# Moving GpSimd's second exit drain ahead of the take of the barrier's arrivals

## The chip, the cores and the metric

One core of a Trainium2 chip. The time is device microseconds (us) of one execution. The "span" is the time from the first to the last recorded instruction of the one execution that was profiled; the measured time of that same execution is 1.78 us longer (82.27 and 80.488 us for the kernel before).

## The reference

A row-wise L2 normalisation of a 1024 x 4096 f32 matrix:

```python
def reference(x, axis, eps):          # x: 1024 x 4096 f32, axis -1, eps 1e-12
    norm = np.sqrt(np.sum(x ** 2, axis=axis, keepdims=True) + eps)
    return (x / norm).astype(np.float32)
```

## The kernel before

The rows are loaded in two transfers of 8.4 MB each, squared and summed on ScalarE and VectorE, scaled in place, and stored in two transfers. All four are issued by SyncE. The part that matters here is what happens after the last store. The program ends with two barriers in which GpSimd takes an arrival from each of the four other engines and then releases them. The kernel before has already edited that exit: the wait for the last store stands at the second barrier, and GpSimd's clean-up (a drain with a reset flag, and a clear of the semaphores that the kernel used) stands inside it.

```python
def one_barrier_behind_last_store(nc, store):
    ...
        everything = take(                     # SyncE's drain that waits for the last store
            lambda i: i.engine == SP and any(w.id == sem for w in waits(i))
        )
        place([everything], lambda i: i.engine == SP and isinstance(i, mybir.InstDrain))
        reset = take(                          # GpSimd's drain with the reset flag
            lambda i: i.engine == POOL
            and isinstance(i, mybir.InstDrain)
            and i.is_reset_sema
        )
        clear = take(lambda i: i.engine == POOL and isinstance(i, mybir.InstISA))
        place(                                 # both in front of the release
            [reset, clear],
            lambda i: i.engine == POOL and isinstance(i, mybir.InstEventSemaphore),
        )
```

`take` removes the first instruction of the last block that fits; `place` inserts ahead of the last one that fits. I listed the last block of both built programs; GpSimd's and SyncE's part of the second barrier is

```
before                                       after
SyncE   drain, waits for the last store      the same
SyncE   drain, signals the arrival           the same
GpSimd  drain                                drain
GpSimd  take (waits for four arrivals)       drain with the reset flag
GpSimd  drain with the reset flag            take (waits for four arrivals)
GpSimd  range clear, semaphores 99 to 104    range clear
GpSimd  release (adds 4)                     release
```

The barrier's own semaphores are 96 (arrivals) and 97 (release).

## Time and profile before

| | before |
|---|---|
| time, median of the first 3 runs | 82.30 us (82.22 to 82.34) |
| span | 80.488 us |
| SyncE sees the last store landed | 79.948 us |
| exit behind that, to the end of the span | 0.540 us |
| time of the profiled execution | 82.27 us |

The page, the waits and the exit line are shown in the prediction. To read them: the DMA queue fills the span, so only what stands behind the store's landing can be shortened by an edit of the exit. One more view belongs here, the exit line's instructions on GpSimd from 57.2 us, just behind the issue of the last store, to the end. The columns are sequencer, operation, count, shortest/median/longest in ns, first and last start in us.

```profile
L251 POOLq EVENT_SEMAPHORE  x4: 17/17/17, 57.2 to 80.4; - x4
L251 POOLq DRAIN  x2: 34/49/64, 57.4 to 80.2; - x2
L251 POOLq EVENT_SEMAPHORE_RANGE_CLEAR  x1: 71/71/71, 80.3 to 80.3; - x1
```

One of the two drains starts at 57.4, the other at 80.2, behind the landing. That second start is the whole subject.

### The profile page before, as it was taken

To read this page: it belongs to the slowest core of one execution; us is meant where nothing else is said; L and a number is where in the kernel's file an instruction comes from. 1 tells how busy PE (TensorE), PEld (TensorE's weight loads), DVE (VectorE), ACT (ScalarE), POOL (GpSimd) and SP (SyncE) were. 2 spreads that over 40 slices of the span, in tenths; PEclk is the share of its full clock that TensorE was granted. 3 is DMA by queue.
4 is the path that set the end of the run, shared out by engine and by line. 5 is a ranking of instruction groups with operands and counts; after the bars stand their busy time and mean duration, and the time that the engine had idled before them with its cause. 6 is when DMAs were issued, how large, how long until landed. Compare 5 with 4: busy or idle time off the path is not lost.

```text
span 80.5 us, 94 instructions
## 1 busy us (share of the span) xinstructions
DVE 27.0 (34%) x21; ACT 29.3 (36%) x23; POOL 0.2 (0%) x4
## 2 busy tenths in 40 slices
DVE  0000000000099599960049995999100000000000
ACT  6000000000099999989149999940000000000000
POOL 0000000000000000000000000000000000000000
DMA  9099999399999399999399999399999399998390
GB/s 489 33 521 521 521 521 391 130 521 521 521 521 391 130 521 521 521 521 391 130 521 521 521 521 391 130 521 521 521 521 391 130 521 521 521 521 358 163 521 0
DMA packets 576, 33.55 MB, mean 417 GB/s; under 512 B 64, under 2 KB 64, under 8 KB 64
## 3 DMA queue, kind: packets, MB, share of 16 engines
q1 hardware_dynamic: 576, 33.55, 97.0%
HBM read 16.78 MB, written 16.78 MB: 417 GB/s over the span
## 4 chain that ended last, share of the span: by engine, by line
DMA 50%; ACT 10%; DVE 9%; issue 0%
DMA xt<-in_x_dram 50%; ACT sq_act L33 9%; DVE xt L64 9%; ACT rstd L53 1%; DVE rstd L59 0%
## 5 line engine op out<-in xcount | busy, mean ns | idle before, releaser
L33 ACT ACTIVATE sq_act<-xt 128x4096 f32<-128x4096 f32 x6 | 21.7, 3610 | 22.8 <-DMA xt<-in_x_dram 22.8
L42 DVE SCALAR_TENSOR_TENSOR sq_dve<-xt 128x4096 f32<-128x4096 f32 x2 | 8.9, 4426 | 26.0 <-DMA xt<-in_x_dram 26.0
L64 DVE TENSOR_SCALAR xt<-xt,rstd 128x4096 f32<-128x4096 f32 x7 | 16.5, 2354 | 0.2
L72 ACT ACTIVATE xt<-xt,rstd 128x3072 f32<-128x3072 f32 x1 | 2.9, 2858 | 0.2 <-DVE rstd L59 0.2
L53 ACT ACTIVATE rstd<-ssq,eps_t 128x1 f32<-128x1 f32 x8 | 2.1, 291 | 0.1
L59 DVE RECIPROCAL rstd<-rstd 128x1 f32<-128x1 f32 x8 | 1.3, 160 | 2.5 <-ACT rstd L53 2.5
L33 ACT ACT_TABLE_LOAD x1 | 1.3, 1283 | 0.8 <-PEq L237 0.8
L53 ACT ACT_TABLE_LOAD x1 | 1.3, 1283 | 0.0
L33 ACT ACTIVATION_READ_ACCUMULATOR sq_act<-xt 128x1 f32 x6 | 1.1, 188 | 0.0
L78 DVE TENSOR_SCALAR xt<-xt,rstd 128x1024 f32<-128x1024 f32 x1 | 0.8, 753 | 0.0
L190 DVE MEMSET eps_t<- 128x1 f32 x1 | 0.1, 59 | 0.9 <-PEq L237 0.9
L42 DVE DVE_READ_ACCUMULATOR sq_dve<-xt 128x1 f32 x2 | 0.2, 83 | 0.0
L237 POOL MEMSET const-bfloat16-1.0<- 128x1 bf16 x1 | 0.1, 102 | 0.0
L237 POOL MEMSET const-uint8-127<- 128x1 uint8 x1 | 0.1, 102 | 0.0
L237 POOL MEMSET const-float32-0.0<- 128x1 f32 x1 | 0.1, 99 | 0.2 <-issue 0.2
L237 POOL MEMSET const-float32-1.0<- 128x1 f32 x1 | 0.1, 99 | 0.0
## 6 DMA issues: line engine op xcount, KB each, us to landing
xt<-in_x_dram SPq DMA_DIRECT2D x2, 31.2
out_dram<-xt SPq DMA_DIRECT2D x2, 22.7
```

Of the source, the lines that this page charges most:

```text
L33: self.nc.scalar.activation(out=sq_a, in_=self.x[:, r], func=ACT_F.Square, accum_out=self.ssq[:, r : r + 1],)
L42: self.nc.vector.scalar_tensor_tensor(out=sq_v, in0=self.x[:, r], scalar=1.0, in1=self.x[:, r], op0=ALU.mult, op1=ALU.mult, accum_out=self ...
L53: self.nc.scalar.activation(out=self.rstd[:, r : r + n], in_=self.ssq[:, r : r + n], func=ACT_F.Sqrt, bias=self.eps_t,)
L59: self.nc.vector.reciprocal(out=self.rstd[:, r : r + n], in_=self.rstd[:, r : r + n])
L64: self.nc.vector.tensor_scalar_mul(out=self.x[:, r], in0=self.x[:, r], scalar1=self.rstd[:, r : r + 1])
L72: self.nc.scalar.activation(out=self.x[:, r, :cut], in_=self.x[:, r, :cut], func=ACT_F.Copy, scale=rstd,)
L78: self.nc.vector.tensor_scalar_mul(out=self.x[:, r, cut:], in0=self.x[:, r, cut:], scalar1=rstd)
L190: nc.vector.memset(eps_t, eps)
L237: nc = _bacc.Bacc("TRN2", target_bir_lowering=False, num_devices=1)
```

## The change

Its intent is to let GpSimd do its second drain while the last store is still on its way.

```diff
+        def semaphore(i):
+            return i.engine == POOL and isinstance(i, mybir.InstEventSemaphore)
+
         reset = take(
             lambda i: i.engine == POOL
             and isinstance(i, mybir.InstDrain)
             and i.is_reset_sema
         )
+        arrival = [n for n, i in enumerate(tail) if semaphore(i)][-2]
+        tail.insert(arrival, reset)
         clear = take(lambda i: i.engine == POOL and isinstance(i, mybir.InstISA))
-        place(
-            [reset, clear],
-            lambda i: i.engine == POOL and isinstance(i, mybir.InstEventSemaphore),
-        )
+        place([clear], semaphore)
```

(Line 251 of the kernel before is line 255 of the changed one.)

## The prediction

> **What bounds the kernel now.** I read the page first, then the chain that ended last, then what the DMA queue's own engine waits for, and last the instructions of the exit line one by one. The page:
>
> ```profile
> span 80.5 us, 94 instructions
> DVE 27.0 (34%) x21; ACT 29.3 (36%) x23; POOL 0.2 (0%) x4
> DMA  9099999399999399999399999399999399998390
> GB/s 489 33 521 521 521 521 391 130 521 521 521 521 391 130 521 521 521 521 391 130 521 521 521 521 391 130 521 521 521 521 391 130 521 521 521 521 358 163 521 0
> q1 hardware_dynamic: 576, 33.55, 97.0%
> ```
>
> The reader should see that no compute engine is busy for more than 36% of the span, while the one DMA queue, which brings in 16.78 MB and sends out 16.78 MB, keeps the 16 DMA engines at work for 97.0% of it. GpSimd has 0.2 us of work, four small memsets at the entry. The chain of waits says the same: of its 18 pieces, the longest is 40.49 us of load from 0.79 us on, and squares, square root, reciprocal and scale fill the stretch up to the last store. The last store is issued at 56.7 us of the span, and from there only the queue works. SyncE's waits show it:
>
> ```profile
> SPq L251 <- DMA out_dram<-xt: 22.4, 2, 19.3
> SPq L251 <- PEq L251: 0.5, 2, 0.4
> ```
>
> SyncE stands 22.4 us at the exit behind the two stores. So the exit has two pieces: a long one in which everybody waits for the transfer, and a short one behind it. Only an instruction of the short piece costs time. The diff moves one instruction of GpSimd from the short piece to the long one, so the whole case is the length of that instruction. The view of the exit line, from 80.03 us to the end at 80.488:
>
> ```profile
> L251 POOLq EVENT_SEMAPHORE  x2: 17/17/17, 80.1 to 80.4; - x2
> L251 SPq DRAIN  x1: 7/7/7, 80.1 to 80.1; - x1
> L251 POOLq DRAIN  x1: 64/64/64, 80.2 to 80.2; - x1
> L251 POOLq EVENT_SEMAPHORE_RANGE_CLEAR  x1: 71/71/71, 80.3 to 80.3; - x1
> L251 SPq EVENT_SEMAPHORE  x1: 17/17/17, 80.4 to 80.4; - x1
> L251 PEldq EVENT_SEMAPHORE  x1: 51/51/51, 80.4 to 80.4; - x1
> ```
>
> The columns are sequencer, operation, count, shortest/median/longest in ns, and first and last start. The starts are rounded to 0.1 us, so I asked the same view for windows of 2 ns and took the window in which each instruction appears and leaves. That gives, in us: SyncE's wait for the store 79.948 to 79.978; its drain that carries the rest of the waits 80.016 to 80.024; its second drain, the arrival, 80.076 to 80.084; GpSimd takes the arrivals 80.108 to 80.126; GpSimd drain 80.190 to 80.254; range clear 80.282 to 80.354; GpSimd's release 80.382 to 80.400; the other four engines leave from 80.424; the last of them, TensorE's queue, ends at 80.488. This is one row: nothing in it lies beside anything else.
>
> **What the Trainium skill says.** "Perfetto Trace Analysis", section "Sequencer-only Instruction (DRAIN, etc)": for such an instruction only its execution is recorded; the wait ahead of it and the spreading of its semaphore update behind it are not. The trace agrees: SyncE's arrival ends at 80.084 and GpSimd's take starts at 80.108, 24 ns in no record, and GpSimd's release ends at 80.400 and the others start at 80.424, again 24 ns. So the price of an instruction is its record plus the gap that goes with it, and I count both. "VectorE: DVE Perf Modes", section "The DRAIN you can't avoid", gives some 12 ns for boilerplate drains on all engines. SyncE's two (7 ns) and TensorE's (8 ns) fit that; GpSimd's do not: 64 ns here, 34 ns at 57.378 and 41 ns at 0.748, so I take the measured ones. "DMA: Bandwidth & Descriptors", where it breaks down the fixed cost of a DMA, puts most of about 2 us down to the confirmation of the last write. Here the records place the last bytes of the store before 77.5 us and SyncE's wait ends at 79.95; whatever the cause, this tail is ahead of the place that the change touches.
>
> **The change part by part.** Nothing is added and nothing is removed; the built programs differ in two places of the last block. Before, GpSimd's order there is: drain, take four arrivals, drain with the reset flag, range clear, release. After: drain, drain with the reset flag, take four arrivals, range clear, release. All waits and updates stay with their instructions. The clear still stands behind the last arrival, so the semaphore that the store counts on is not cleared early.
>
> Step 1, where the drain goes. GpSimd's first exit drain is at 57.378 to 57.412. The moved one follows it, at about 57.47 (the two SyncE drains in a row lie 52 ns apart). It takes 34 to 64 ns and is done by about 57.54. GpSimd then has nothing to do until the take at 80.108. So the moved drain costs 0 on the path, with 22.5 us to spare.
>
> Step 2, what leaves the path. From the end of the take to the start of the clear it is now 80.282 - 80.126 = 156 ns: a gap of 64, the drain of 64, a gap of 28. The drain's 64 ns go. Of the two gaps one stays, and which one is the choice I have to make. Behind an event-semaphore instruction GpSimd has gaps of 60 ns (57.236 to 57.296, to another one), 64 ns (57.314 to 57.378, to a drain) and 64 ns (80.126 to 80.190). At the entry it is 60 ns again (0.608 to 0.668). Behind the drain and behind the clear it is 28 ns each. So the gap goes with the instruction in front, whatever follows, and behind the take it stays at 60 to 64 ns. What is saved is the drain and the gap behind it: 64 + 28 = 92 ns.
>
> Step 3, what follows. Clear, release and the leaving of the other engines keep their lengths and move forward as a block. The span becomes 80.488 - 0.092 = 80.396 us. The time is the span plus what lies outside it: 82.30 - 80.49 = 1.81 us by the median, and no part of that is touched. Sum: 82.30 - 0.09 = 82.21 us, or 0.11% less.
>
> **Rivals.** First, the gap in front of the clear turns out to be the short one: then 64 + 64 = 128 ns are saved and the time is 82.17 us. For it: the clear did start 28 ns after what stood in front of it. Against it: three other intervals behind event-semaphore instructions, all of 60 ns or more.
>
> Second, the drain's 64 ns are partly the price of waking up after 22 us of waiting, because the two earlier exit and entry drains took 34 and 41 ns. Then whatever comes first after the take pays the extra 23 to 30 ns, now the clear, and 62 to 69 ns are saved: 82.23 to 82.24 us. For it: 64 is the longest of the three. Against it: the drain at the entry behind the memsets took 181 ns, so the length varies with what is in flight. I can't exclude it.
>
> Third, the range clear needs an idle GpSimd and waits out by itself what the drain waited out. Then the clear grows and the gain is near 0: 82.30 us. Against it: GpSimd has executed nothing since the four memsets that end at 0.43 us, and there is nothing left to wait out.
>
> Fourth, a loss: for example, that SyncE or another engine's arrival becomes later. No arrival depends on GpSimd's second drain; the last of the other engines' arrivals, TensorE's at 57.502, comes 22.6 us before SyncE's. I see no route to more than a few ns.
>
> All four lie within 0.13 us of the time before, and the three times of the kernel before span 82.22 to 82.34, also 0.12 us. The load and the stores, 97% of the span, can wander more between executions than the whole change is worth: 0.1% of 80 us is 0.08 us.
>
> **Range and chances.** Centre 82.21 us. The mechanism alone gives 82.17 to 82.30. I widen it by the spread of the runs before, about 0.1 us up and slightly more down for another chip or another placement in memory: 82.03 to 82.38. Two per cent would be 1.65 us, over three times the whole exit behind the store's landing (80.488 - 79.948 = 0.54 us), so faster by 2% is impossible by this change and slower by 2% would need a disturbance. I give 1% to each and 98% to within 2%.
>
> **What the changed profile would show.** Step 1 is right if GpSimd shows two drains between 57.3 and 57.7 us and none after 80 us. Step 2 is right if the clear starts 60 to 64 ns after the end of the take; 28 ns would be the first rival; a clear longer than 71 ns, or a gap over 80 ns, the second or third. Step 3 is right if from the landing seen by SyncE to the end it is about 0.45 us in place of 0.54 us. This difference is the one to look at: the total span moves with the transfers and can hide it. I would be wrong in kind if the clear grew by as much as the drain took, or if the exit were as long as before.

## The result, and the profile after

The changed kernel took 82.16 us (median of 6 runs, 82.08 to 82.36) against 82.29 us before (6 runs, 82.21 to 82.35). Ratios here are the mean time of one kernel's fast runs over that of the other's of the same rounds, so not quite the ratio of the medians; it is 0.999 with a 95% interval of 0.9975 to 1.0005. The interval includes 1: the medians and ratios alone do not prove that anything changed. The trace does. The page after:

```profile
span 80.6 us, 94 instructions
DMA  9299999399999399999399999399999399999390
q1 hardware_dynamic: 576, 33.55, 96.9%
```

SyncE's waits after:

```profile
SPq L255 <- DMA out_dram<-xt: 22.5, 2, 19.3
SPq L255 <- PEq L255: 0.5, 2, 0.3
```

The exit line on GpSimd, from 57.2 us to the end:

```profile
L255 POOLq EVENT_SEMAPHORE  x4: 17/17/17, 57.3 to 80.5; - x4
L255 POOLq DRAIN  x2: 34/49/64, 57.5 to 57.6; - x2
L255 POOLq EVENT_SEMAPHORE_RANGE_CLEAR  x1: 71/71/71, 80.4 to 80.4; - x1
```

Both drains now start before 57.7, and their lengths are what they were, 34 and 64 ns. The exit line from 80.21 us, behind SyncE's first drain, to the end:

```profile
L255 POOLq EVENT_SEMAPHORE  x2: 17/17/17, 80.3 to 80.5; - x2
L255 SPq DRAIN  x1: 7/7/7, 80.3 to 80.3; - x1
L255 POOLq EVENT_SEMAPHORE_RANGE_CLEAR  x1: 71/71/71, 80.4 to 80.4; - x1
...
L255 PEldq EVENT_SEMAPHORE  x1: 51/51/51, 80.5 to 80.5; - x1
```

The row of the kernel before had a GpSimd drain between the two event semaphores; this one has none, and the clear has kept its 71 ns. Located to 2 ns in the way that the prediction describes, the exit divides like this:

| piece of the exit, us | before | after |
|---|---|---|
| SyncE sees the store landed | 79.948 | 80.132 |
| from there to the start of GpSimd's take | 0.160 | 0.160 |
| start of the take to the start of the clear | 0.174 | 0.080 |
| start of the clear to the end of the span | 0.206 | 0.208 |
| exit, sum | 0.540 | 0.448 |

The span itself grew, from 80.488 to 80.580 us, because the profiled execution of the changed kernel was one of its two slowest (82.36 us). Its loads landed later: the load piece of the chain, which ends with the second load, is 40.61 us where it was 40.49. SyncE's drain behind the issue of the last store, its arrival at the first barrier, starts at 57.178 where it was 57.064 (+0.114), and the store landed 0.184 later, so the transfer of the store gave another 0.07. Then the exit gave back 0.092: 0.184 - 0.092 = 0.092 us of net growth. The change touches no instruction ahead of the last store's issue, and in the eight later profiles the landing moves about too, from 79.836 to 80.030 us; the 80.132 of the changed kernel is the latest of the ten. The eight alone spread over 0.19 us, twice the effect. So the exit, not the span, is the quantity to compare.

Whether the exit's gain reaches the measured time can be read from the same executions. The time of a profiled execution, less the moment at which SyncE sees the landing, leaves the wander of the transfers out: 82.27 - 79.948 = 2.32 us before, 82.36 - 80.132 = 2.23 us after. So the 0.09 us are in the measured time as well, and what lies outside the span has stayed at 1.78 us.

### The profile page after: what moved, and what is told of

Its sections match the earlier page's. It is cut to its first block, busy times and chain, and to the rows that moved or that the text cites. A ratio compares the mean times of both kernels' runs of the same rounds, so it can differ in the third digit from the quotient of the medians.

```text
span 80.6 us, 94 instructions
## 1 busy us (share of the span) xinstructions
DVE 27.0 (34%) x21; ACT 29.3 (36%) x23; POOL 0.2 (0%) x4
## 4 chain that ended last, share of the span: by engine, by line
DMA 50%; ACT 10%; DVE 9%; issue 0%
DMA xt<-in_x_dram 50%; ACT sq_act L33 9%; DVE xt L64 9%; ACT rstd L53 1%; DVE rstd L59 0%
```

## The experiments

My theory: an instruction on GpSimd's row costs its record and one gap while it stands between the take and the release, and nothing ahead of the take. The rivals: the drain's 64 ns are the price of waking up after a long wait, and would fall on whatever comes first (A); the exit is bound by something else (B); the exit's gain does not reach the measured time (C). The first four kernels ran on one chip, the second four on another. In each of the two sets, the kernel before ran beside them (7 and 11 runs, medians 82.29 and 82.25 us). All outputs were correct.

**Twenty drains behind the take.** Edit of the kernel before:

```diff
+        extra = [mybir.InstDrain(name=f"I-{90000 + n}", engine=POOL) for n in range(20)]
         place(
-            [reset, clear],
+            [*extra, reset, clear],
```

> Twenty extra plain GpSimd drains between the take of the arrivals and the drain with the reset flag, in the kernel before. Theory (a drain behind the take costs its record and one gap, in full): each extra drain 34 ns + 28 ns = 62 ns, 1.24 us in all; from the end of SyncE's wait for the store to the end of the span 0.54 + 1.24 = 1.78 us; time 82.29 + 1.24 = 83.5 us, ratio about 1.015. Rival A (drains with nothing to drain are cheap and only the first after a long wait is dear, as a wake-up): the first of them takes 64 ns, the others far less, and the one with the flag, no longer first, falls from 64 to about 34 ns; well under 1 us in all.

83.49 us (83.38 to 83.96, 4 runs), ratio 1.0152, interval 1.0119 to 1.0184. The exit is 1.756 us. GpSimd's part of the exit line behind the landing:

```profile
L252 POOLq EVENT_SEMAPHORE  x2: 17/17/17, 80.0 to 81.5; - x2
L252 POOLq DRAIN  x1: 64/64/64, 81.3 to 81.3; - x1
```

No view of the trace lists the extra drains, probably because, made by hand, they carry no source line; they show as the time between the take's end at 80.014 and the start of the flagged drain at 81.294. That is 1.280 us, less the gap of 64 ns that was there before: 1.216 us for twenty, 61 ns each. The flagged drain, now last of 21, still takes 64 ns, so its length is no wake-up. The price of an instruction on this row is paid in full, and it reaches the measured time: the medians differ by 1.20 us. Rival A fails, and rival C fails for an effect of this size.

**The same twenty drains ahead of the take.** Edit of the changed kernel:

```diff
-        tail.insert(arrival, reset)
+        extra = [mybir.InstDrain(name=f"I-{90000 + n}", engine=POOL) for n in range(20)]
+        tail[arrival:arrival] = [*extra, reset]
```

> The same twenty extra drains ahead of the take, in the changed kernel. Theory (what GpSimd does ahead of the take lies beside the store's transfer): they run from about 57.5 to 58.8 us, the take stays where SyncE's arrival puts it, the exit behind SyncE's wait is 0.448 us as in the changed kernel, time 82.2 us, ratio to before 0.999 and 1.2 us under the run with the drains behind. Rival B (the place does not matter, because the exit is bound by something else than GpSimd's row): same time as the run with the drains behind.

82.15 us (82.12 to 82.26, 4 runs), ratio 0.9976, interval 0.9959 to 0.9993, which excludes 1 and includes the 0.9989 of the theory; it does not show that this kernel is faster than the changed one. The exit is 0.446 us. GpSimd from 57.2 us to the end:

```profile
L256 POOLq DRAIN  x2: 34/49/64, 57.4 to 58.7; - x2
L256 POOLq EVENT_SEMAPHORE_RANGE_CLEAR  x1: 71/71/71, 80.3 to 80.3; - x1
```

The flagged drain has moved to 58.7 us behind the twenty, and nothing at the end has moved. The same work costs 1.2 us on one side of the take and nothing on the other. Rival B fails.

**The two drains ahead of the take exchanged.** Edit of the changed kernel:

```diff
-        tail.insert(arrival, reset)
+        tail.insert(arrival - 1, reset)
```

> The changed kernel with GpSimd's two exit drains ahead of the take exchanged: the one with the reset flag first, the plain one second. If the 64 ns belong to the flag: first drain 64 ns, second 34 ns. If they belong to the place (second of a pair, or what stands in front): first 34, second 64. Either way the exit behind SyncE's wait stays at 0.448 us.

One run, 82.19 us, exit 0.446 us. GpSimd in the window from 57.3 to 57.48 us:

```profile
L255 POOLq DRAIN  x1: 64/64/64, 57.4 to 57.4; - x1
```

and from 57.48 to 57.6 us:

```profile
L255 POOLq DRAIN  x1: 34/34/34, 57.5 to 57.5; - x1
```

The 64 ns go with the flagged drain, not with the place.

**The plain drain behind the take, a first attempt.** Edit of the changed kernel:

```diff
-        place([clear], semaphore)
+        plain = tail.pop(arrival - 1)
+        assert plain.engine == POOL and isinstance(plain, mybir.InstDrain)
+        place([plain, clear], semaphore)
```

> The changed kernel with the plain drain put behind the take, so that each of the two drains has the other's place of the kernel before. Theory with the flag as owner of the 64 ns: the plain drain takes 34 ns with a gap of 64 ahead and 28 behind; the exit is 0.448 + 0.062 = 0.510 us. Rival A (the first drain after 22 us of waiting is dear): it takes 64 ns, the exit is 0.540 us, as in the kernel before.

One run, 82.25 us. The exit was 0.540 us with a drain of 64 ns behind the take, which looked like rival A. It was a mistake of mine. Taking the clear out shortens the list by one ahead of `arrival`, so `arrival - 1` was the flagged drain, and my check did not look at the flag. The listing of the built program showed the order of the kernel before. The run is thus an unplanned repeat of that kernel: the exit is 0.540 us again, with a landing at 79.928.

**The plain drain behind the take, mended.** The instruction is now found by its name:

```diff
+        first = tail[arrival - 1]
         tail.insert(arrival, reset)
...
-        place([clear], semaphore)
+        plain = take(lambda i: i.name == first.name)
+        place([plain, clear], semaphore)
```

> What the run before meant to do and did not: the drain with the flag ahead of the take, the plain drain behind it. If the 64 ns belong to the flag, as the exchanged pair says: plain drain 34 ns, gap 64 ahead and 28 behind, exit 0.448 + 0.062 = 0.510 us. If to the wait ahead of it: 64 ns and 0.540 us.

One run, 82.16 us. GpSimd from 80.0 us to the end:

```profile
L257 POOLq EVENT_SEMAPHORE  x2: 17/17/17, 80.0 to 80.3; - x2
L257 POOLq DRAIN  x1: 34/34/34, 80.1 to 80.1; - x1
```

The exit is 0.510 us, from 79.868 to 80.378, with gaps of 64 ns ahead of the drain and 28 behind it: 34 + 28 = 62 ns over the changed kernel. A drain that comes first after the long wait takes 34 ns if it has no flag. This settles rival A against it.

**The changed kernel again.**

> The changed kernel as it is, for a tighter ratio. Theory: 92 ns less, ratio 0.9989; the exit behind SyncE's wait for the store 0.448 us whatever the transfers did before it. Rival C (the six runs differ only by the transfers, and the exit does not reach the measured time): the ratio is 1.000 with the interval around it.

82.24 us (82.07 to 82.33, 6 runs) beside 82.25 us before, ratio 0.9988, interval 0.9966 to 1.0009. The exit is 0.448 us again (79.932 to 80.380). The ratio is the expected 0.9989 to a digit, but the interval still includes 1. The expected effect is about a third of the spread of single runs, and more rounds of the same would narrow this only slowly. For the 92 ns themselves, the ratio does not exclude rival C. The profiled executions do: from the landing to the end of the measured time are 2.24 us here and 2.23 in the first profile of the changed kernel, 2.23 in the two others with the same exit, and 2.32 in both executions with the order of the kernel before (table below).

**The clear behind the release.** Semaphores 99 to 104, which it clears, are waited on by nobody once all have arrived, and the barrier's own are not among them. Edit of the changed kernel:

```diff
-        place([clear], semaphore)
+        tail.append(clear)
```

> The changed kernel with the range clear behind GpSimd's release (it clears semaphores 99 to 104, the barrier's are 96 and 97, and nobody waits on a cleared one behind the arrivals). Theory (an instruction of GpSimd's row costs its record and one gap while it stands ahead of the release, and beside the others' leaving it costs only what sticks out): release 60 ns behind the take, TensorE's queue ends 88 ns behind the release; the clear starts 60 to 64 ns behind the release, takes 71 and ends the span, 210 ns behind the end of the take in place of 270: exit 0.388 us, 60 ns under the changed kernel, ratio to before about 0.998. Rival: the clear behind a release is slower or waits for the others, and the exit is 0.448 us or more.

82.15 us (82.08 to 82.35, 6 runs), ratio 0.9983, interval 0.9959 to 1.0007. GpSimd from 80.0 us to the end:

```profile
L255 POOLq EVENT_SEMAPHORE  x2: 17/17/17, 80.1 to 80.2; - x2
L255 POOLq EVENT_SEMAPHORE_RANGE_CLEAR  x1: 71/71/71, 80.3 to 80.3; - x1
```

The release ends at 80.194, TensorE's queue at 80.282, the clear at 80.328. So the clear now lies beside the leaving of the other engines and sticks out by 46 ns. The exit is 0.390 us, 58 ns under the changed kernel.

The span got shorter, but not the time. In the profiled execution, 82.17 - 80.328 = 1.84 us lie outside the span, where the changed kernel has 1.78 and 1.79. With the span to 0.1 us, as every run lists it, the mean is 1.85 us over the six runs here, against 1.79 over the six of the changed kernel and 1.79 over the eleven of the kernel before. From the landing to the end of the measured time are 2.23 us, as in the changed kernel. So the theory, that the clear costs only what sticks out behind the others, held for the span and failed for the time: rival C is true of this step. A possible reason is that what follows the span waits for GpSimd, which still has the same instructions to do; no run tests that.

**One SyncE drain in place of two, on top of that.** The arrival's drain gets the waits of the other as well, so no wait is lost:

```diff
-        place([everything], lambda i: i.engine == SP and isinstance(i, mybir.InstDrain))
+        at = max(
+            n
+            for n, i in enumerate(tail)
+            if i.engine == SP and isinstance(i, mybir.InstDrain)
+        )
+        arrive = tail[at]
+        tail[at] = mybir.InstDrain(
+            name=arrive.name,
+            engine=SP,
+            sync_info=mybir.SyncInfo(
+                on_wait=[*waits(arrive), *waits(everything)],
+                on_update=arrive.sync_info.on_update,
+            ),
+        )
```

> The one before, and SyncE's two exit drains made one that holds the waits of both and signals the arrival. Theory: 60 ns of SyncE's row (80.016 to 80.076 in the kernel before) leave the path as well: exit 0.33 us, ratio to before about 0.9973. Rival: the waits of two drains on one need one more event-semaphore instruction ahead of it, behind the last landing, and the exit stays at 0.388 us or grows.

82.06 us (82.00 to 82.18, 6 runs), ratio 0.9968, interval 0.9948 to 0.9989, which excludes 1. The take starts 0.100 us after SyncE sees the landing (80.008 to 80.108) instead of 0.160; the exit is 0.332 us. The merged drain itself has no record (it was made by hand, like the twenty). GpSimd from 80.0 us to the end:

```profile
L268 POOLq EVENT_SEMAPHORE  x2: 17/17/17, 80.1 to 80.2; - x2
L268 POOLq EVENT_SEMAPHORE_RANGE_CLEAR  x1: 71/71/71, 80.3 to 80.3; - x1
```

It looks like the one before, because the saving lies ahead of the take. It has 0.208 us less exit than the kernel before and 0.19 us less by the medians. But 0.06 us of that exit come from the clear behind the release, and again 1.84 us lie outside the span. From the landing to the end of the time are 2.17 us: 0.15 us less than before, 0.09 from the change of this document and 0.06 from SyncE's drain. Against the changed kernel in the same set the mean is 82.07 to 82.23 us; a plain two-sample interval of mine for that difference, from six runs of each, is 0.05 to 0.27 us.

All exits side by side, from SyncE's sight of the landing to the end of the span, and at the right the time of the same execution and what of it lies behind the landing:

| kernel | landing seen | end | exit | expected by the theory | time | time less landing |
|---|---|---|---|---|---|---|
| before | 79.948 | 80.488 | 0.540 | | 82.27 | 2.32 |
| after | 80.132 | 80.580 | 0.448 | 0.45 | 82.36 | 2.23 |
| twenty drains behind | 79.836 | 81.592 | 1.756 | 1.78 | 83.38 | 3.54 |
| twenty drains ahead | 80.030 | 80.476 | 0.446 | 0.448 | 82.26 | 2.23 |
| drains exchanged | 79.962 | 80.408 | 0.446 | 0.448 | 82.19 | 2.23 |
| order of before (the mistake) | 79.928 | 80.468 | 0.540 | 0.510, for the order that was meant | 82.25 | 2.32 |
| plain drain behind | 79.868 | 80.378 | 0.510 | 0.510 | 82.16 | 2.29 |
| after, again | 79.932 | 80.380 | 0.448 | 0.448 | 82.17 | 2.24 |
| clear last | 79.938 | 80.328 | 0.390 | 0.388 | 82.17 | 2.23 |
| one SyncE drain, clear last | 80.008 | 80.340 | 0.332 | 0.33 | 82.18 | 2.17 |

## Why the prediction was right

- **What bounds the kernel.** Right: the transfers fill the span before and after, and the exit in its two pieces is what the experiments moved.
- **Step 1, the drain costs nothing ahead of the take.** Right. It starts at 57.552, 26 ns behind the first drain, where I had taken 52 ns from SyncE's pair, and is done at 57.618; the take is 22.7 us later. Even twenty more beside it cost nothing.
- **Step 2, 64 + 28 ns leave the path.** Right, with the choice of the gap that stays: the clear starts 62 ns behind the end of the take (80.310 to 80.372), so the gap belongs to the instruction in front. The exit shrank by 92 ns.
- **Step 3, the rest moves as a block.** Right in the exit (0.206 before, 0.208 after). The measured median, 82.16 us, is 0.05 us under the predicted 82.21 and inside the range. What lies outside the span, 1.78 us in the same execution, was not touched. That the median came so near is partly luck: the range, 0.35 us wide, is nearly four times the effect and also covers no effect at all (82.30 us), so the time could not have told. The exit does.
- **Rivals.** The short gap and the growing clear did not come. The second, which I could not exclude, that 64 ns contain a wake-up, was wrong: flagged drains take 64 ns wherever they stand, unflagged ones 34 ns at the exit. The entry's 181 ns, which I held against this rival, decide nothing: that drain does not stand behind the memsets but beside them (0.300 to 0.481 us, the last memset to 0.431), and I did not test it.
- **What I passed over.** I wrote that the clear still stands behind the last arrival. But the flagged drain, in the built program, names a reset range too, semaphores 99 to 104, and it now runs ahead of SyncE's last waits. SyncE still waits there for 99 (until 80.132 us) and for 102 (until 80.200), VectorE's and ScalarE's counts, which were full before the last store was issued. Had the drain cleared them at 57.6 us, nothing was left to fill them again and SyncE would have hung. It did not, and the outputs of this kernel's second set were correct, so the drain cleared neither. The prediction did not ask this.
- **What I read from the Trainium skill.** That SyncE's two drains fit its 12 ns leaves out SyncE's first exit drain, 129 ns (57.064 to 57.193). The breakdown of a DMA's fixed cost stands in the page's section on transfers issued through GpSimd, while these are SyncE's; nothing in the argument rests on it.

What stays open: why the drain with the flag is 30 ns longer, what makes the transfers' end wander, and why the clear behind the release saves no time. A slower store is not quite excluded as a side effect: from the start of its issue to the landing it takes 23.27 to 23.32 us in the three profiles with the flagged drain behind the take, 23.27 to 23.35 in the seven others, means 0.03 us apart. Against it stands that twenty more drains ahead of the take (23.34 us) add nothing to that of the changed kernel (23.35 and 23.32). The ratio of the change alone is not resolved by its runs; its 0.09 us are read from the exit and from the time behind the landing.

## What to carry to other kernels

An engine that waits at a barrier for the last store has the whole transfer to do its clean-up in: whatever needs only that engine's own work to be finished belongs ahead of the take. Check first what it could disturb: here, the semaphores that the others still wait on. Work moved behind the release shortened the span by 0.06 us here and the time not at all, so compare the measured time of the profiled execution too. Price such an instruction by its record plus the gap behind it, and compare the piece of the trace that the edit touches, not the span, when the transfers wander by more than the edit is worth. If an effect is too small for the clock, repeat the suspect twenty times on each side of the wait.

## What the Trainium skill lacked or had wrong

- "VectorE: DVE Perf Modes", section "The DRAIN you can't avoid", gives some 12 ns for the boilerplate drains that the runtime adds on all five engines, and nothing for a program's own barrier drains, which these are. At the exit GpSimd's recorded drains took 34 ns without the reset flag and 64 ns with it, in every profile; SyncE's took 129 ns behind the issue of the store and 7 at the end, TensorE's 7 to 8, ScalarE's 14, VectorE's 19.
- "Perfetto Trace Analysis", section "Sequencer-only Instruction (DRAIN, etc)", names the hidden tail of such an instruction but no size. Here it is 24 ns from the end of GpSimd's release to the start of the first engine that leaves, and GpSimd's gap to its own next instruction is 60 to 64 ns behind an event semaphore, 26 to 28 ns behind a drain or a range clear.
- No page that I found prices the exit barrier of the program itself: 0.540 us from the landing seen to the end, and 0.332 us in the last version, whose clear behind the release shortens the span alone.
